# Two scaling multiplies of a memory attention: on VectorE in place of GpSimd

## Chip, cores and metric

One core of a Trainium2 chip runs the whole kernel. The metric is the device time of one execution in microseconds (us), lower is better. The core's engines, as the profile names them: PE (TensorE matmul; PEld its weight loads), DVE (VectorE), ACT (ScalarE), POOL (GpSimd) and SP (SyncE, which here only issues DMAs). Each engine works through its own queue in order and waits on semaphores for the others.

## What is computed

One layer of an encoder trunk on a sequence of 2048 tokens, 1024 channels, in float32. In the reference it has three parts: forgetting attention beside a multi-scale pool, then attention to 256 memory tokens, then a SwiGLU. The middle one matters here:

```python
hn = rmsnorm(h, g_mem_q)
mq = rmsnorm(head_split(hn @ w_mem_q, 4, 128), g_q_mem)      # queries, 4 heads of 128
sc = einsum('bshd,bmhd->bhsm', mq, mk) * 128 ** -0.5         # mk: 256 memory keys per head
pm = softmax(sc)
mo = einsum('bhsm,bmhd->bshd', pm, mv)
h = h + mo @ w_mem_out
```

## The kernel before

Float32 matmuls are made of three products of a high and a low word: a value x is split into `hi` (a rounded copy, written by ACT) and `lo = x - hi` (a subtraction on DVE, L55), and `mm3` issues hi·hi, hi·lo and lo·hi (L60 to L62). A DVE instruction on line L55 is therefore nearly always the second half of such a split, and the third matmul of a triple (L62) waits for it.

The memory attention takes the sequence in 16 tiles of 128 tokens, called 0 to 15 here. Tiles 0 and 1 begin in the stage before. From tile 2 on, one loop over n does in step n a piece of several tiles at once, in this order on PE:

- `query_norm` of tile n: 24 matmuls into a PSUM bank `mmps`. ACT scales it into `mq` (L1212) and squares it (L1214). DVE sums the squares per head (`ms`, L1216). POOL turns the four sums of each row into reciprocal roots `r` (L67, L71). Then `mq` is multiplied by `r`, 128x512 with `r` broadcast over each head (L1219).
- `ffn_turn` of tile n-5: PE transposes, DVE evicts them to `hst` (L1103), POOL stores `hst` (L1104).
- for every second n, `mem_values` of a pair of tiles (`mops`).
- the scores of tile n-1 (`scps`), then `softmax`: DVE takes the negated maxima `ng` (L1238), ACT four exponentials with their sums `l` (L1241), DVE the reciprocals of the sums (L1242), and `pm` is multiplied by them, 128x1024 with `l` broadcast over each head (L1243).
- `weights_tm` of tile n-2: eight transposes of `pm` (PE), high words by ACT (L1041), low words `pTl` by DVE (L55).
- `mem_out` of tile n-4, first half; DVE adds the residual (L1443).
- `tile_query` of tile n+1: eight transposes of `h`, whose high and low words go to one of three places named `hT`, `qs` and `kh` in turn. These are what `query_norm` of step n+1 reads.
- `mem_out`, second half, and last `query_t`: four transposes of the scaled `mq` of tile n.

The transposes use PSUM buffers `tp`, two in turn, and a transpose into a buffer waits until the DVE instruction that read it last is done. In the last steps the loop also takes in work of the stage behind it: sums of token blocks on DVE (`xraw`, L1074, with their splits into `qs`, `kh`, `kl`, `cb`) and of the first gate weights (`graw`, `t`, L1134), all from SBUF.

In this loop the orders of PE and SP are those of the code. DVE, ACT and POOL are ordered by a list scheduler when the kernel is built, so moving an instruction to another engine can move its neighbours.

Of the kernel before, what the change touches and what calls it, by code (L numbers as in the profile page):

```python
# [11 lines left out]
ALU = mybir.AluOpType  # L12
# [4 lines left out]
P = 128  # L17
# [9 lines left out]
MEM = 256  # L27
MH = 4
# [12 lines left out]
def block_kernel(ctx: ExitStack, tc: tile.TileContext, x, xT, memT, cols, rows, w_qkvf, w_p, w_pool, w_out,  # L41
# [4 lines left out]
    act, dve, pool, pe, sp = nc.scalar, nc.vector, nc.gpsimd, nc.tensor, nc.sync  # L46
# [10 lines left out]
    def mm3(ps, st, mv, first, last, goes_on=False):  # L57

        (sh, sl), (mh, ml) = st, mv
        pe.matmul(ps, lhsT=sh, rhs=mh, start=first, stop=False, skip_group_check=goes_on)  # L60
        pe.matmul(ps, lhsT=sh, rhs=ml, start=False, stop=False, skip_group_check=goes_on)  # L61
        pe.matmul(ps, lhsT=sl, rhs=mh, start=False, stop=last, skip_group_check=goes_on)  # L62

    def rsqrt(outp, ms, inv_n=None):

        if inv_n is not None:
            pool.tensor_scalar(out=ms, in0=ms, scalar1=inv_n, scalar2=EPS, op0=ALU.mult, op1=ALU.add)  # L67
        else:
            pool.tensor_scalar(out=ms, in0=ms, scalar1=EPS, scalar2=None, op0=ALU.add)
        n = ms.shape[-1]  # L70
        pool.tensor_tensor(out=outp, in0=ms, in1=mhalf[:, :n], op=ALU.pow)  # L71
# [1136 lines left out]
    def query_norm(ps, r, hTh, hTl):  # L1208
        for k in range(KD):
            mm3(ps, (hTh[:, k], hTl[:, k]), wq[k], k == 0, k == KD - 1)  # L1210
        mq = hp.tile([P, MH, P], F32, tag="cm", name="mq", bufs=3)
        act.activation(mq[:].rearrange("p h d -> p (h d)"), ps, AF.Copy, scale=r)  # L1212
        sq = hp.tile([P, MH, P], F32, tag="cm", name="mqsq", bufs=3)
        act.activation(sq[:], mq[:], AF.Square)  # L1214
        ms4 = stat.tile([P, MH], F32, tag="ms4", name="ms4", bufs=2)
        dve.tensor_reduce(out=ms4[:], in_=sq[:], axis=AX.X, op=ALU.add)  # L1216
        r4 = stat.tile([P, MH], F32, tag="r4", name="r4", bufs=2)
        rsqrt(r4[:], ms4[:], 1.0 / P)
        pool.tensor_tensor(out=mq[:], in0=mq[:], in1=r4[:].unsqueeze(2).to_broadcast([P, MH, P]), op=ALU.mult)  # L1219
        return mq  # L1220

    def query_t(mq, bank=tp_bank):
# [7 lines left out]
    def softmax(scs, pm, mqh, mql):  # L1230

        nh = MH // len(scs)
        sc = [s_[:, h] for s_ in scs for h in range(nh)]
        for h in range(MH):
            mm3(sc[h], (mqh[:, h], mql[:, h]), (mk[0][:, h], mk[1][:, h]), True, True)
        ng = stat.tile([P, MH], F32, tag="ng4", name="ng4", bufs=2)
        for n, s_ in enumerate(scs):
            dve.tensor_reduce(out=ng[:, n * nh:(n + 1) * nh], in_=s_, axis=AX.X, op=ALU.max, negate=True)  # L1238
        l4 = stat.tile([P, MH], F32, tag="l4", name="l4", bufs=2)
        for h in range(MH):  # L1240
            act.activation(pm[:, h], sc[h], AF.Exp, bias=ng[:, h:h + 1], scale=1.0, accum_out=l4[:, h:h + 1])  # L1241
        dve.reciprocal(l4[:], l4[:])  # L1242
        pool.tensor_tensor(out=pm[:], in0=pm[:], in1=l4[:].unsqueeze(2).to_broadcast([P, MH, MEM]), op=ALU.mult)  # L1243
        return pm

    with ExitStack() as c0:
# [98 lines left out]
        with in_order(EN.SP):  # L1345
# [46 lines left out]
            queries[1]()  # L1392
            mqd, qtd, pmd = {}, {}, {}
            mqd[0] = query_norm(banks[0], *qd.pop(0))
            earlier_1(*prev)
            mqd[1] = query_norm(banks[0], *qd.pop(1))
            qtd[0] = query_t(mqd.pop(0))
            pm0 = f(pair_place(6)[:]).rearrange("p a (h m) -> p (a h) m", m=MEM)
            pmd[0] = softmax([b_.rearrange("p (h m) -> p h m", m=MEM) for b_ in banks[1:]], pm0, *qtd.pop(0))
            queries[2]()  # L1400
            earlier_2(*prev)
            qtd[1] = query_t(mqd.pop(1))

    with mstack, ExitStack() as c0:
# [67 lines left out]
        with in_order(EN.SP):  # L1472
# [5 lines left out]
            for n in range(2, NT + 1):  # L1478
                if n < NT:
                    mqd[n] = query_norm(bigp.tile([P, 512], F32, tag="mm", name="mmps", bufs=2)[:], *qd.pop(n))  # L1480
# [16 lines left out]
                if 0 <= i < NT:  # L1497
                    pmd[i] = ptp.tile([P, MH, MEM], F32, tag="pm", name="pm", bufs=2)
                    softmax([bigp.tile([P, MH, MEM], F32, tag="sc", name="scps", bufs=1)[:]], pmd[i][:], *qtd.pop(i))
# [328 lines left out]
```

## Time and profile before

| | |
|---|---|
| median of 3 runs | 2586.41 us (2582.59 to 2586.48) |
| profiled execution, its own time | 2578.56 us |
| its span, first to last instruction | 2576.9 us |
| PE busy | 2510.7 us, 97% of the span |
| DVE busy | 1734.8 us, 67% |
| ACT busy | 1299.4 us, 50% |
| POOL busy | 822.0 us, 32% |
| the 16 `mq` multiplies (L1219), POOL | from 1024.9 to 1261.3 us of the span, 17.0 us in all |
| the 16 `pm` multiplies (L1243), POOL | from 1035.4 to 1277.2 us, 30.2 us in all |

Times within the execution are counted from the start of the span. Matmuls overlap in the pipe: a row's duration is longer than the distance to the next row's start, and the same holds, by less, for DVE rows that follow each other. The profiled execution took 7.85 us less than the median of the runs.

### The profile page before, as it was taken

The page shows a single profiled execution, that of the slowest core. Times are in us where ns is not written, and L with a number is a line of the kernel's source. Part 1 is how long each engine was busy: PE and PEld are TensorE (multiplying, and loading weights), DVE is VectorE, ACT ScalarE, POOL GpSimd, SP SyncE. Part 2 cuts the span into 40 slices and gives each one's busy share as a digit, 9 for nine tenths or more (in the row PEclk, how much of TensorE's full clock was granted, in tenths as well). Part 3 has the DMA queues.
Part 4 walks back from the last instruction along what each step waited for, and adds up shares of the span by engine and source line. Part 5 has one row for each costly group of instructions (what it writes and reads, how often), then busy time and mean ns, then how long its engine had stood idle before and what let it go on. Part 6 is the DMA issues. An engine that isn't in the chain of part 4 may idle for free.

```text
span 2576.9 us, 37301 instructions
## 1 busy us (share of the span) xinstructions
PE 2510.7 (97%) x12909; PEld 2154.4 (84%) x12909; DVE 1734.8 (67%) x2998; ACT 1299.4 (50%) x2487; POOL 822.0 (32%) x1135
## 2 busy tenths in 40 slices
PE   8999998999999899999999999999999999999998
PEld 8999997788887687888778888888888888888887
DVE  4466745899998754555877778756766666665554
ACT  5555446788889422655543433334543333333443
POOL 0022424455555522444424545430001222212000
PEclk9999999999999999999999999999999999999999
DMA  8755767645433546222465555447773323325665
GB/s 276 215 178 156 216 192 210 187 123 156 130 109 92 185 150 214 74 87 95 174 224 181 174 178 190 151 164 271 244 266 109 122 104 108 122 98 185 228 214 186
DMA packets 246766, 434.01 MB, mean 168 GB/s; under 512 B 30000, under 2 KB 119856, under 8 KB 238896
## 3 DMA queue, kind: packets, MB, share of 16 engines
q1 hardware_dynamic: 213104, 322.54, 39.5%
q0 software_dynamic: 33472, 109.08, 11.7%
q8 instruction: 102, 1.67, 0.3%
q14 instruction: 88, 0.72, 0.1%
HBM read 294.02 MB, written 137.50 MB: 167 GB/s over the span
## 4 chain that ended last, share of the span: by engine, by line
PE 49%; issue 8%; DVE 2%; ACT 1%; DMA 1%; POOL 1%; SPq 0%; POOLq 0%; DVEq 0%; ACTq 0%
PE bk L62 13%; PE bk L60 13%; PE bk L61 13%; PE mmps L60 2%; PE mmps L62 2%; PE mmps L61 2%; PE tp L1039 1%; DVE ww L55 0%; PE obk L60 0%; PE obk L61 0%; PE obk L62 0%; DMA xraw<-hTd 0%; POOL out_dram L1721 0%; DMA wqr<-in_w_mem_q_dram 0%; DMA h<-h1d 0%
## 5 line engine op out<-in xcount | busy, mean ns | idle before, releaser
L55 DVE TENSOR_TENSOR ww<-draw,ww 128x512 fp32r<-128x512 f32 x308 | 205.2, 702 | 155.6 <-ACT ww L199 155.1
L199 ACT CAST ww<-draw 128x512 fp32r<-128x512 f32 x308 | 179.5, 620 | 218.8 <-PE bk L62 174.5
L55 DVE TENSOR_TENSOR ww<-graw,ww 128x512 fp32r<-128x512 f32 x220 | 177.8, 815 | 105.9 <-ACT ww L199 105.5
L61 PE MATMUL bk<-ww,ww 128*128 128x512 f32 x616 | 239.6, 389 | 0.0
L60 PE MATMUL bk<-ww,ww 128*128 128x512 f32 x616 | 239.6, 389 | 0.0
L62 PE MATMUL bk<-ww,ww 128*128 128x512 f32 x616 | 239.6, 389 | 0.0
L199 ACT CAST ww<-graw 128x512 fp32r<-128x512 f32 x220 | 135.9, 622 | 181.8 <-PE bk L62 159.8
L55 DVE TENSOR_TENSOR pl<-tp,ph 128x512 fp32r<-128x512 f32 (+3 forms) x296 | 176.7, 599 | 27.8 <-ACT ph L952 26.0
L871 ACT ACTIVATE s<-s,mx 128x1024 f32<-128x1024 f32 (+2 forms) x192 | 173.6, 905 | 7.7 <-DVE mx L865 7.1
L936 PE MATMUL tp<-ident,s 128*128 128x128 f32 x1088 | 171.5, 273 | 3.4 <-DVE pl L55 3.0
L60 PE MATMUL zps<-wh,xhi 128*128 128x386 f32 x512 | 174.6, 341 | 0.0
L62 PE MATMUL zps<-wh,xl 128*128 128x386 f32 x512 | 173.7, 339 | 0.0
L61 PE MATMUL zps<-wl,xhi 128*128 128x386 f32 x512 | 173.2, 338 | 0.0
L952 ACT CAST ph<-tp 128x512 fp32r<-128x512 f32 (+3 forms) x296 | 148.7, 514 | 38.3 <-PE tp L936 32.8
L936 PEld LDWEIGHTS tp<-ident,s 128*128 128x128 f32 x1088 | 133.9, 141 | 31.6 <-DVE pl L55 6.6
L1721 POOL DMA_DIRECT2D out_dram<-o x32 | 17.3, 542 | 382.5 <-DVE o L1718 381.6
L62 PE MATMUL bk<-qs,ww 128*128 128x512 f32 x352 | 137.2, 390 | 1.1 <-DVE ww L55 1.1
L60 PE MATMUL bk<-qs,ww 128*128 128x512 f32 x352 | 137.9, 392 | 0.3 <-ACT s L1640 0.3
L61 PE MATMUL bk<-kh,ww 128*128 128x512 f32 x352 | 137.0, 389 | 0.0
L60 PE MATMUL bk<-kl,ww 128*128 128x512 f32 x352 | 136.9, 389 | 0.0
L61 PE MATMUL bk<-cb,ww 128*128 128x512 f32 x352 | 136.9, 389 | 0.0
L62 PE MATMUL bk<-kl,ww 128*128 128x512 f32 x352 | 136.9, 389 | 0.0
(613 smaller groups left out, 7261.9 us busy)
## 6 DMA issues: line engine op xcount, KB each, us to landing
graw<-in_w_gu_dram SPq DMA_DIRECT2D x44, 1024.0 KB, 5.4
draw<-in_w_down_dram SPq DMA_DIRECT2D x66, 256.0 KB, 4.3
xl<-in_xT_dram SPq DMA_DIRECT2D x64, 256.0 KB, 4.5
wdr<-in_w_down_dram SPq DMA_DIRECT2D x22, 512.0 KB, 4.6
jl<-in_x_dram SPq DMA_DIRECT2D x32, 256.0 KB, 7.0
vd<-cb SPq DMA_DIRECT2D x16, 512.0 KB, 3.5
cb<-cd SPq DMA_DIRECT2D x8, 1024.0 KB, 7.8
v<-vd SPq DMA_DIRECT2D x8, 1024.0 KB, 5.4
```

The lines of the kernel that those rows point to most:

```text
L55: (eng or dve).tensor_tensor(out=lo, in0=src, in1=f(hi), op=ALU.subtract)
L60: pe.matmul(ps, lhsT=sh, rhs=mh, start=first, stop=False, skip_group_check=goes_on)
L61: pe.matmul(ps, lhsT=sh, rhs=ml, start=False, stop=False, skip_group_check=goes_on)
L62: pe.matmul(ps, lhsT=sl, rhs=mh, start=False, stop=last, skip_group_check=goes_on)
L199: act.copy(hi, raw)
L871: act.activation(s[:, sl], s[:, sl], AF.Exp, bias=ng, scale=-1.0, accum_out=l[:, q, g:g + 1])
L936: pe.transpose(tp[:, q * P:(q + 1) * P], unit["rows"][q][:, j * P:(j + 1) * P], ident[:])
L952: act.copy(ph[:, sl], tp[:, sl])
L1039: pe.transpose(tp[:, e_], src[:, q + e_], ident[:])
L1721: pool.dma_start(out[rows_, cs], o)
```

## The change

Both multiplies are given to DVE instead of POOL; operands, shapes and places stay.

```diff
@@ query_norm
         rsqrt(r4[:], ms4[:], 1.0 / P)
-        pool.tensor_tensor(out=mq[:], in0=mq[:], in1=r4[:].unsqueeze(2).to_broadcast([P, MH, P]), op=ALU.mult)
+        dve.tensor_tensor(out=mq[:], in0=mq[:], in1=r4[:].unsqueeze(2).to_broadcast([P, MH, P]), op=ALU.mult)
         return mq
@@ softmax
         dve.reciprocal(l4[:], l4[:])
-        pool.tensor_tensor(out=pm[:], in0=pm[:], in1=l4[:].unsqueeze(2).to_broadcast([P, MH, MEM]), op=ALU.mult)
+        dve.tensor_tensor(out=pm[:], in0=pm[:], in1=l4[:].unsqueeze(2).to_broadcast([P, MH, MEM]), op=ALU.mult)
         return pm
```

The reciprocal roots `r` are still made on POOL. The orders of PE and SP are the same as before. POOL loses 32 instructions. DVE gains 32, and the scheduler puts them as follows.

DVE at tile 3, as it stands with the change (`wm30l` is the low word of a weight, `qs` are the low words that `query_norm` of tile 4 reads):

```order
L1216 TENSOR_REDUCE ms_13219<-mqsq 128x4
L55 TENSOR_TENSOR wm30l<-wmr,wm30h 128x512
L1219 TENSOR_TENSOR mq<-mq,r_13221 128x512
L1238 TENSOR_REDUCE ng_13241<-scps 128x4
L55 TENSOR_TENSOR pTl<-tp_13250,pTh 128x4x128
L55 TENSOR_TENSOR pTl<-tp_13257,pTh 128x4x128
L55 TENSOR_TENSOR qs<-tp_13271,qs 128x512
L55 TENSOR_TENSOR qs<-tp_13278,qs 128x512
```

The `mq` multiply is new in this list; all else stands as before, now behind it. At tile 2 it stands behind `ng` and ahead of the two `pTl` and of `hT`.

DVE at tile 11, one of the tiles with odd numbers in the even part of the loop (5, 7, 9, 11 and 13 read alike), the difference:

```order
 L1216 TENSOR_REDUCE ms_14551<-mqsq 128x4
 L1103 TENSOR_TENSOR hst<-tp_14565,gffn 128x512
+L1219 TENSOR_TENSOR mq<-mq,r_14553 128x512
 L1238 TENSOR_REDUCE ng_14589<-scps 128x4
 L55 TENSOR_TENSOR pTl<-tp_14598,pTh 128x4x128
 L55 TENSOR_TENSOR pTl<-tp_14605,pTh 128x4x128
+L1443 TENSOR_TENSOR h_13352<-mmps,h_13352 128x512
 L1242 RECIPROCAL l_14591<-l_14591 128x4
-L1443 TENSOR_TENSOR h_13352<-mmps,h_13352 128x512
+L1243 TENSOR_TENSOR pm<-pm,l_14591 128x1024
 L55 TENSOR_TENSOR hT<-tp_14633,hT 128x512
 L55 TENSOR_TENSOR hT<-tp_14640,hT 128x512
```

`mq` now stands ahead of `ng`, and `pm` ahead of the low words of the next tile's `hT`.

DVE at tile 15, the last query, the difference:

```order
 L1103 TENSOR_TENSOR hst<-tp_15241,gffn 128x512
 L1216 TENSOR_REDUCE ms_15235<-mqsq 128x4
-L55 TENSOR_TENSOR kh<-xraw,qs 128x512
+L1238 TENSOR_REDUCE ng_15290<-scps 128x4
+L1219 TENSOR_TENSOR mq<-mq,r_15237 128x512
 L1103 TENSOR_TENSOR hst<-tp_15249,gffn 128x512
-L1238 TENSOR_REDUCE ng_15290<-scps 128x4
 L55 TENSOR_TENSOR pTl<-tp_15299,pTh 128x4x128
```

`ng` and `mq` have come between the sum of squares and the second `hst`, and a `kh` has gone from there to a place earlier.

## Prediction

> **What bounds the kernel.** I read the page first, then the busy time in the stretch that holds the two multiplies, then PE's own waits there.
>
> ```profile
> PE 2510.7 (97%) x12909; PEld 2154.4 (84%) x12909; DVE 1734.8 (67%) x2998; ACT 1299.4 (50%) x2487; POOL 822.0 (32%) x1135
> ...
> 1062.00:1244.00 182.00, 181.00 (x1069) 157.50 (x1067) 95.81 (x142) 104.15 (x225) 83.87 (x116) 1.00 0.29 97
> 1244.00:1300.00 56.00, 49.26 (x270) 40.31 (x269) 49.27 (x74) 29.09 (x65) 22.76 (x29) 1.00 0.57 203
> ```
>
> The last two rows give, after the length, busy us of PE, PEld, DVE, ACT and POOL, then the granted clock. PE is the bound of the whole kernel. From 1062 to 1244 it leaves 1.0 us of 182 free, with DVE only 53% busy; from 1244 to 1300 it leaves 6.7 us, and DVE is the busiest engine beside it (88%). The clock is 1.00 in both, so only PE's waits can change. PE's waits from 1000 to 1320 (total us, times, longest):
>
> ```profile
> PE tp L1039 <- POOL mq L1219: 3.6, 2, 2.0
> PE tp L1039 <- DVE hst L1103: 2.8, 6, 1.8
> PE mmps L60 <- DVE ww L1443: 2.2, 1, 2.2
> ...
> PE tp L1039 <- POOL hr L71: 1.2, 1, 1.2
> ...
> PE tp L1102 <- DVE pTl L55: 0.8, 1, 0.8
> ```
>
> PE waits for `mq` only twice in 16 tiles, and never for `pm`. The gain can't be 16 times anything; what counts is what the two instructions delay on DVE.
>
> **Prices of the moved instructions.** The POOL rows of the multiplies, and a DVE row of the stage before with the same form as `pm` (128x1024 by a broadcast factor from POOL):
>
> ```profile
> L1243 POOL TENSOR_TENSOR pm<-pm,l 128x1024 f32<-128x1024 f32 x15 | 28.3, 1890 | 26.8 <-PE mmps L62 18.3 <-DVE l L1242 8.5
> L1219 POOL TENSOR_TENSOR mq<-mq,r 128x512 f32<-128x512 f32 x16 | 17.0, 1060 | 1.3
> ...
> L411 DVE TENSOR_TENSOR cb<-kh,zrq 128x1024 f32<-128x1024 f32 x8 | 9.8, 1222 | 7.7 <-POOL zrq L71 7.7
> ```
>
> So `pm` costs 1.22 us on DVE against 1.89 on POOL, and `mq` 0.68 (the 128x512 rows below) against 1.06. In a run of DVE rows the next starts after 0.60 (128x512) or 1.13 (128x1024), and these are what a queue pays. For the step from POOL to DVE and from DVE to PE I take 0.07 us each (at tile 15 below, `hst` ends at 1260.64 and PE starts at 1260.70). POOL gets 47 us back (17.0 and 30.2); apart from `mq`, PE waits for POOL only in the one row on `hr`, which is taken up below, so this relief is costed at nothing by itself.
>
> **Tile 2.** The rows around PE's first wait, by engine:
>
> ```profile
> 1045.27 1.03 POOL L71 TENSOR_TENSOR r<-ms,mhalf 128x4 f32<-128x4 f32 x1
> 1044.81 1.21 DVE L1238 TENSOR_REDUCE ng<-scps 128x4 f32<-128x1024 f32 x1
> 1045.94 1.28 DVE L55 TENSOR_TENSOR pTl<-tp,pTh 128x512 fp32r<-128x512 f32 x2
> 1047.14 0.68 DVE L55 TENSOR_TENSOR hT<-tp,hT 128x512 fp32r<-128x512 f32 x1
> 1047.47 0.66 PE L1039 MATMUL tp<-ident,mq 128*128 128x128 f32 x4 [1.64 <-POOL mq L1219]
> 1048.42 0.39 PE L62 MATMUL mmps<-qs,hT 128*128 128x512 f32 x1
> ```
>
> `r` ends at 1046.30, so `mq` runs on DVE from 1046.37 to 1047.05 and PE starts its transposes at 1047.12: 0.35 earlier. But DVE stands still from 1045.94 until `r` comes, and both `pTl` and `hT` are behind `mq`: `hT` begins at 1046.37 + 3 x 0.60 = 1048.17 and ends at 1048.85. The third matmul of the next tile (L62, 1048.42) needs it, so it starts at 1048.92. The gain is gone and PE is **0.5 us later**.
>
> **Tile 3.** The same with `mq` ahead of `ng` too:
>
> ```profile
> 1056.57 1.01 POOL L71 TENSOR_TENSOR r<-ms,mhalf 128x4 f32<-128x4 f32 x1
> 1056.35 1.22 DVE L1238 TENSOR_REDUCE ng<-scps 128x4 f32<-128x1024 f32 x1
> 1058.68 1.28 DVE L55 TENSOR_TENSOR qs<-tp,qs 128x512 fp32r<-128x512 f32 x2
> 1058.75 0.66 PE L1039 MATMUL tp<-ident,mq 128*128 128x128 f32 x4 [1.97 <-POOL mq L1219]
> 1059.71 0.39 PE L62 MATMUL mmps<-qs 128*128 128x512 f32 x1
> ```
>
> `r` ends at 1057.58, `mq` runs from 1057.65, PE's transposes gain 0.35 again. `ng` waits from 1056.35 to 1058.25, then 1.13 for `ng` and 2 x 0.60 for `pTl` put `qs` at 1060.58 to 1061.26, and the L62 matmul of tile 4 at 1061.33 in place of 1059.71: **1.6 us later**.
>
> **Tiles 4 to 13.** In even tiles `r` comes while DVE is idle or in a split with slack; I cost them at nothing, because the matmuls of `mem_values` and of the scores stand on PE between and hide `mq`; without that cover they would cost what an odd tile costs. The same holds for tiles 0 and 1, for whose `mq` PE does not wait now. In odd tiles `ng` waits for `r`:
>
> ```profile
> 1188.04 1.04 POOL L71 TENSOR_TENSOR r<-ms,mhalf 128x4 f32<-128x4 f32 x1
> 1188.13 1.21 DVE L1238 TENSOR_REDUCE ng<-scps 128x4 f32<-128x1024 f32 x1
> 1191.53 1.04 PE L1039 MATMUL tp<-ident,h 128*128 128x128 f32 x8
> ```
>
> `mq` starts at 1189.15, `ng` at 1189.75 (1.6 late), the two `pTl` at 1190.88 and 1191.48, the second ending at 1192.16. PE's eight transposes of `h` reuse the two `tp` buffers that the `pTl` free. The first four, at 1191.53, would wait 0.1, the second four, at 1191.97, up to 0.26. The cover of 1.6 us is just used up. Between 0 and 0.26 I take 0.14 for each of five odd tiles, since the margin is that of my hops: **0.7 us**. `pm` lands in idle time: the exponentials and the `hT` behind them move with `ng`, and the transposes of `mq` at the end of the step still find `hT` done. If that cover is gone, each `pm` is worth at most its 1.13 us.
>
> **From 1238 on** DVE is nearly full, and two effects work against each other. Rows:
>
> ```profile
> 1238.26 1.04 POOL L71 TENSOR_TENSOR r<-ms,mhalf 128x4 f32<-128x4 f32 x1
> 1246.13 2.60 DVE L1074 TENSOR_TENSOR xraw<-xraw 128x512 f32<-128x512 f32 x1
> 1246.26 1.91 POOL L1243 TENSOR_TENSOR pm<-pm,l 128x1024 f32<-128x1024 f32 x1
> 1248.65 1.28 DVE L55 TENSOR_TENSOR hT<-tp,hT 128x512 fp32r<-128x512 f32 x2
> 1249.47 0.63 PE L1039 MATMUL tp<-ident,mq 128*128 128x128 f32 x4 [1.22 <-POOL hr L71]
> 1249.85 0.68 DVE L1074 TENSOR_TENSOR xraw<-xraw 128x512 f32<-128x512 f32 x1
> ...
> 1239.72 1.53 DVE L55 TENSOR_TENSOR cb<-xraw,kl 128x512 fp32r<-128x512 f32 x1
> 1264.76 1.86 DVE L55 TENSOR_TENSOR kh<-xraw,qs 128x512 fp32r<-128x512 f32 x1
> 1277.51 2.10 DVE L55 TENSOR_TENSOR cb<-xraw,kl 128x512 fp32r<-128x512 f32 x1
> ```
>
> The same `xraw` subtraction takes 0.68 us alone and 2.60 while POOL's `pm` (1246.26 to 1248.17) runs: a DVE instruction with two operands in SBUF stands still as long as POOL's multiply works. Four such rows lose 1.92, 0.85, 1.18 and 1.42 us over 0.68, 5.4 in all. The change ends these and pays 3 x 1.13 + 2 x 0.60 = 4.6 on DVE. [...]
>
> *Before 1249.47:* PE waits for a `tp` buffer that `hT` frees (ended 1249.33). With the change `mq` begins when `r` is there, at 1239.37, and from it to `hT` DVE has eleven instructions at 0.60 (`mq`, two `ww`, two `kh`, `cb`, two `pTl`, two `xraw`, `h`), two at 1.13 (`ng`, `pm`) and a reciprocal at 0.1: 9.0 us. That puts `hT` at 1248.3 in place of 1248.65: **-0.3 us**. The `hr` that the list names ended at the same moment; without `pm` ahead of it on POOL it comes earlier too.
>
> *Tile 15.* The second `hst` frees the `tp` buffer for `pm`:
>
> ```profile
> 1259.96 0.68 DVE L1103 TENSOR_TENSOR hst<-tp,gffn 128x512 f32<-128x512 f32 x1
> 1260.18 1.04 POOL L71 TENSOR_TENSOR r<-ms,mhalf 128x4 f32<-128x4 f32 x1
> 1260.70 0.65 PE L1039 MATMUL tp<-ident,pm 128*128 128x128 f32 x4 [1.75 <-DVE hst L1103]
> ```
>
> Now it stands behind `mq`, and so behind `r`, which ends at 1261.22: `mq` at 1261.29, `hst` at 1261.89 to 1262.57, PE at 1262.64: **+1.9 us**.
>
> *1261 to 1291:* two blocked rows (1.18 + 1.42) go and two `pm` (2 x 1.13) come. DVE's work is 0.3 us less. PE arrives 1.9 later by the step before, while its waits here come to 1.5 at most (the 6.7 us left free, less 1.2, 1.8 and 2.2 of the rows for `hr`, `hst` and L1443; the longest is the 0.8 for `pTl`): they can go, no more. Between 0 and -1.5 I take **-1.0**, since the delay is longer than the waits.
>
> *The end of the stage:*
>
> ```profile
> 1294.92 0.69 DVE L1134 TENSOR_TENSOR t<-graw,t 128x512 f32<-128x512 f32 x1 [3.00 <-DMA hTd<-hst]
> 1297.33 1.28 DVE L1443 TENSOR_TENSOR ww<-mmps,ww 128x512 f32<-128x512 f32 x2
> 1298.07 0.50 PE L60 MATMUL mmps<-wm00h,ww 128*128 128x512 f32 x1 [2.18 <-DVE ww L1443]
> ```
>
> DVE waits 3.0 us for a store, then does four instructions, then the L1443 that PE waits for. In the new order six stand between, 1.2 us more, if the store moves with PE (it holds `hst`, which follows PE's transposes). If it hangs on other stores of POOL's queue instead, PE is late enough to find it landed, and loses its 2.2 of waiting. Between -2.2 and +1.2 I take **0**, near the middle, as no row decides.
>
> **Sum:** 0.5 + 1.6 + 0.7 - 0.3 + 1.9 - 1.0 + 0 = +3.4 us. The profiled execution's span goes from 2576.9 to 2580.3 and its time from 2578.56 to about 2582.0; the median lies 7.85 above that execution, which gives 2589.8. A difference under 0.2% (5.2 us) can't be told from none here, so the forecast is no measurable change, leaning to slower.
>
> **Rivals.** [...] PE's 6.7 free us from 1244 to 1300 hang on DVE or on what DVE delays. If the 5.4 us that DVE gets back remove them all and tile 15 costs nothing, the sum is 0.5 + 1.6 + 0.7 - 6.7 = -3.9: 2582.5. For it: the four long rows. Against: `hst` of tile 15 waits for `r` whatever DVE's load. It decides if `r` of tile 15 is ready by 1260. [...] *C, every step gains.* If each multiply were on PE's path, 16 x (1.06 - 0.68) + 16 x (1.89 - 1.22) = 16.8 us would go: 2569.6. The list of waits speaks against it: two of 32 are. [...]
>
> **How the numbers follow.** Forecast 0.60, A 0.13 (0.03 of it beyond -0.2%), B 0.22, C 0.05. Faster is C and the tail of A, 0.08; slower is B, 0.22; the rest, 0.70, is the same. The range goes from just under A, 2582.0, to B, 2595.0; left out are C, the tail of A and about half of B, 0.19. The forecast's own range is 2586.4 to 2591.6.
>
> **What would show it.** L1219 and L1243 on DVE at about 0.68 and 1.22 us; no PE wait for `mq` from POOL, but waits at L62 for `hT` and `qs` of 0.5 to 2 us at tiles 2 to 4; `ng` of odd tiles behind a DVE wait for `r`; no `xraw` row over 1 us from 1240 to 1280; PE's wait for `hst` at tile 15 near 3.5 us. The forecast is wrong if the L62 waits stay away, if PE's waits from 1249 to 1298 vanish, or if they grow beyond 10 us.

## The result: 0.23% slower, and where it went

Over twelve runs each the changed kernel takes 2590.79 us (2582.71 to 2594.62) and the kernel before 2584.66 us (2580.55 to 2589.65). The ratio is 1.0023, with a 95% interval of 1.0015 to 1.0032: 6.1 us slower, where 3.4 us were forecast. The forecast time was 2589.8 us, which looks closer than it is: it stood on a median of before that was 1.75 us above the one of twelve runs. So the difference is what has to be explained.

The page of the changed kernel, its line of busy times, and below it the two stretches of the loop (length, busy us of PE, PEld, DVE, ACT and POOL, granted clock, DMA). The second stretch is a little longer than the one of before, since everything comes later:

```profile
PE 2516.2 (97%) x12909; PEld 2157.6 (83%) x12909; DVE 1754.6 (68%) x3030; ACT 1300.5 (50%) x2487; POOL 777.7 (30%) x1103
...
1062.00:1244.00 182.00, 179.83 (x1047) 154.59 (x1048) 109.86 (x161) 105.43 (x229) 54.90 (x93) 1.00 0.27 89
1244.00:1310.00 66.00, 58.10 (x312) 48.79 (x311) 54.55 (x86) 32.59 (x71) 17.86 (x27) 0.95 0.59 211
```

POOL is 44 us lighter and DVE 20 us heavier, and that decides nothing. Two things do: PE leaves more time free, and the granted clock of the second stretch is 0.95 where it was 1.00. The two instructions themselves, by group (count, busy us, mean ns, then the idle time of DVE just before them):

```profile
L1243 DVE TENSOR_TENSOR pm<-pm,l 128x1024 f32<-128x1024 f32 x15 | 18.4, 1224 | 0.4
L1219 DVE TENSOR_TENSOR mq<-mq,r 128x512 f32<-128x512 f32 x16 | 11.1, 692 | 13.2 <-POOL r L71 13.2
```

Both cost what was forecast (1.22 and 0.69 us, for 1.22 and 0.68). `pm` finds its operand ready. Ahead of `mq` DVE stands still for 13.2 us in all, and whatever is queued behind it stands too. PE's waits from 1000 to 1330 show who that was:

```profile
PE tp L1039 <- DVE hst L1103: 4.6, 7, 3.2
PE mmps L60 <- DVE ww L1443: 3.1, 1, 3.1
PE tp L1039 <- DVE mq L1219: 2.9, 2, 1.6
PE mmps L62 <- DVE qs L55: 1.7, 1, 1.7
...
PE tp L1039 <- DVE hT L55: 0.8, 1, 0.8
...
PE mmps L62 <- DVE hT L55: 0.6, 1, 0.6
```

The waits for `mq` are shorter than those for POOL's `mq` (2.9 for 3.6). In exchange PE waits for `hT` (0.6, at L62) and `qs`, which it did not before, and longer for `hst` (4.6 us for 2.8).

**Tile 3** in the rows of DVE, POOL and PE:

```profile
1058.42 1.01 POOL L71 TENSOR_TENSOR r<-ms,mhalf 128x4 f32<-128x4 f32 x1
1059.46 0.69 DVE L1219 TENSOR_TENSOR mq<-mq,r 128x512 f32<-128x512 f32 x1 [1.18 <-POOL r L71]
1060.07 1.22 DVE L1238 TENSOR_REDUCE ng<-scps 128x4 f32<-128x1024 f32 x1
1061.21 1.28 DVE L55 TENSOR_TENSOR pTl<-tp,pTh 128x512 fp32r<-128x512 f32 x2
1062.40 1.28 DVE L55 TENSOR_TENSOR qs<-tp,qs 128x512 fp32r<-128x512 f32 x2
1063.14 0.50 PE L62 MATMUL mmps<-qs 128*128 128x512 f32 x1 [1.74 <-DVE qs L55]
```

DVE idles 1.18 us for `r`; `ng`, `pTl` and `qs` follow, and PE waits 1.74 us at the third matmul of tile 4, where 1.6 had been worked out.

**Tile 15**, where the second `hst` frees PE's `tp` buffer, and the first matmuls behind it:

```profile
1264.58 1.04 POOL L71 TENSOR_TENSOR r<-ms,mhalf 128x4 f32<-128x4 f32 x1
1265.65 0.69 DVE L1219 TENSOR_TENSOR mq<-mq,r 128x512 f32<-128x512 f32 x1 [0.70 <-POOL r L71]
1266.26 0.68 DVE L1103 TENSOR_TENSOR hst<-tp,gffn 128x512 f32<-128x512 f32 x1
1267.10 1.08 PE L1039 MATMUL tp<-ident,pm 128*128 128x128 f32 x4 [3.20 <-DVE hst L1103]
...
1268.40 0.63 PE L61 MATMUL mmps<-wm00l,ww 128*128 128x512 f32 x1
1268.83 0.63 PE L62 MATMUL mmps<-wm00h,ww 128*128 128x512 f32 x1
1269.26 0.63 PE L60 MATMUL mmps<-wm10h,ww 128*128 128x512 f32 x1
```

The wait of 3.20 us is the forecast one. What was not forecast stands below it: these 128x512 matmuls start 0.43 us apart, while the same matmuls elsewhere in this stage start 0.227 apart. The stretches around this wait and around the one at the stage's end, in periods of 3.41 us (columns as above):

```profile
1262.96:1266.37 3.41, 0.66 (x4) 0.42 (x4) 2.71 (x5) 2.11 (x9) 1.99 (x3) 1.00 0.98 380
1266.37:1269.79 3.42, 2.69 (x9) 2.34 (x10) 3.42 (x6) 2.16 (x6) 1.37 (x2) 0.50 0.93 342
1300.50:1303.92 3.42, 0.83 (x4) 0.37 (x2) 3.42 (x7) 1.24 (x2) 0.00 (x0) 1.00 1.03 379
1303.92:1307.33 3.41, 2.93 (x7) 2.35 (x8) 1.02 (x2) 0.00 (x0) 0.55 (x1) 0.50 1.01 386
```

In the first and third row PE was busy for 0.66 and 0.83 of 3.41 us. In the next 3.41 us the granted clock is exactly half. No such stretch lies between 973 and 1330 in the profiled execution of before.

**The account by stretch.** The distance on PE between the same two matmuls, after less before, from 1036 to 1326 of before. The clock's part is half of the time that PE worked at half clock; it is taken out of the four stretches and stands by itself.

| kernel (profiled execution) | 1036-1062 | 1062-1244 | 1244-1292 | 1292-1326 | without clock | clock |
|---|---|---|---|---|---|---|
| the change | +2.1 | +1.2 | -0.7 | +0.9 | +3.6 | +2.8 |
| forecast | +2.1 | +0.7 | +0.6 | 0 | +3.4 | none |

So in this execution the queue cost what was forecast, and the clock came on top: 6.4 us together, 6.1 in the medians. The split is not exact, since a PE that the clock has delayed waits less elsewhere. The kernel e11 below has the same order of work up to 1292, and half-clock stretches at tiles 2 and 3 that cost it 4.8 us; its first three columns are +1.8, +1.0 and -1.5, so the queue's part up to 1292 is between 1.4 and 2.7 us.

The clock's part does not rest on single executions alone, because the granted clock of every run is on record. One less the clock, times the span, is the time that the clock takes if PE works all the while. In the mean it is 19.5 us over 35 runs of before and 23.5 over the twelve of the change, 4.0 more with an uncertainty of 1.0. In the half-clock rows above PE worked 2.69 and 2.93 us of 3.41, so about four fifths of that, some 3 us (an estimate), are lost time of PE.

### The profile page after: what moved, and what is told of

Same layout as the page of the kernel before. It is cut to its first block, busy times and chain, and to the rows that moved or that the text cites. A ratio compares the mean times of both kernels' runs of the same rounds, so it can differ in the third digit from the quotient of the medians.

```text
span 2585.5 us, 37240 instructions
## 1 busy us (share of the span) xinstructions
PE 2516.2 (97%) x12909; PEld 2157.6 (83%) x12909; DVE 1754.6 (68%) x3030; ACT 1300.5 (50%) x2487; POOL 777.7 (30%) x1103
## 4 chain that ended last, share of the span: by engine, by line
PE 49%; issue 9%; DVE 2%; POOL 1%; ACT 1%; DMA 1%; POOLq 0%; DVEq 0%; ACTq 0%
PE bk L62 13%; PE bk L61 13%; PE bk L60 13%; PE mmps L62 2%; PE mmps L60 2%; PE mmps L61 2%; PE tp L1039 1%; DVE ww L55 0%; PE obk L60 0%; DMA wqr<-in_w_mem_q_dram 0%; PE obk L61 0%; PE obk L62 0%; POOL out_dram L1721 0%; DVE hst L1103 0%; ACT mq L1212 0%
## 5 line engine op out<-in xcount | busy, mean ns | idle before, releaser
L62 PE MATMUL bk<-ww,ww 128*128 128x512 f32 x616 | 239.6, 389 | 0.0
L62 PE MATMUL zps<-wh,xl 128*128 128x386 f32 x512 | 173.7, 339 | 0.0
L62 PE MATMUL bk<-qs,ww 128*128 128x512 f32 x352 | 137.2, 390 | 1.2 <-DVE ww L55 1.2
L62 PE MATMUL bk<-kl,ww 128*128 128x512 f32 x352 | 136.9, 389 | 0.0
L61 PEld LDWEIGHTS bk<-ww,ww 128*128 128x128 f32 x616 | 115.6, 188 | 24.4 <-DVE ww L55 0.4
```

## The experiments

Two theories for the loss. *Q, the queue:* DVE works in order and stands still for POOL's `r`; the loss is what stands behind `mq`. *L, the load:* the loss is DVE's added work, two thirds of it `pm`. For the second half of the loss a third theory, *K, the clock*, with what speaks for and against it below. In the tables "measured" is the ratio to the kernel before with its 95% interval, and in us of 2584; the stretches are as above.

**One multiply at a time.** The first kernel moves only `mq`, the second only `pm` (each is before with one line of the change).

```diff
-        pool.tensor_tensor(out=mq[:], in0=mq[:], in1=r4[:]...)    # first kernel: mq only
+        dve.tensor_tensor(out=mq[:], in0=mq[:], in1=r4[:]...)
-        pool.tensor_tensor(out=pm[:], in0=pm[:], in1=l4[:]...)    # second kernel: pm only
+        dve.tensor_tensor(out=pm[:], in0=pm[:], in1=l4[:]...)
```

Expected of `mq` alone:

> Only the multiply of mq (L1219) goes to VectorE; that of pm (L1243) stays on GpSimd. Theory Q (queue): the loss of the whole change comes from VectorE standing still for r in its in-order queue, so this half alone loses: the waits of PE for hT at tile 2 and qs at tile 3 (0.6 and 1.7 us in the whole change) and the one of about 3.2 us for hst at tile 15 stay, the long xraw and kh rows from 1240 on stay too; +4 to +6 us, ratio 1.0015 to 1.0025. Theory L (load): the loss is VectorE's added work, 16 x 0.60 us here against 16 x 1.13 us of the other half, so about a third of the +6.1 us, +2 us, ratio 1.0008.

Expected of `pm` alone:

> Only the multiply of pm (L1243) goes to VectorE; that of mq (L1219) stays on GpSimd. Theory Q: nothing new waits for r on VectorE, the rows that the multiply of pm held up (1.92, 1.18 and 1.42 us) go, PE's wait for hst at tile 15 is at most 1.8 us; -1 to -3 us, ratio 0.999 to 1.000. Theory L: two thirds of the loss, +4 us, ratio 1.0016.

| kernel | measured | 1036-1062 | 1062-1244 | 1244-1292 | 1292-1326 | without clock | clock |
|---|---|---|---|---|---|---|---|
| `mq` only | 1.0024 (1.0014 to 1.0034), +6.2 | +1.1 | +1.1 | +1.2 | 0.0 | +3.5 | +3.4 |
| `pm` only | 1.0006 (0.9997 to 1.0014), +1.5 | +0.6 | -0.1 | -0.9 | +1.6 | +1.3 | +3.4 |

`mq` alone loses as much as both, and L's 1.0008 lies outside its interval. That settles for Q. `pm` alone did not gain the 1 to 3 us that Q gave it. The +0.6 of its first stretch is a queue too: the first of the 16 multiplies of `pm` now stands ahead of two `kh`, and PE waits 0.57 us for these at 1040.30. PE's longest waits of that kernel from 1244 to 1310 show where they stayed:

```profile
PE mmps L60 <- DVE ww L1443: 3.9, 1, 3.9
PE tp L1039 <- DVE hst L1103: 1.8, 1, 1.8
```

The wait at tile 15 keeps its 1.8, the 0.9 us are gained up to 1292, and the stage's end gives them back: its wait grows from 2.18 to 3.9 us. DVE gets its `t` there only after 3.66 us of waiting for the store, and then six instructions stand ahead of L1443, as in the changed kernel, instead of four.

**The last tile.** The whole change, with `mq` of tile 15 left on POOL.

```diff
-    def query_norm(ps, r, hTh, hTl):
+    def query_norm(ps, r, hTh, hTl, eng=None):
-        dve.tensor_tensor(out=mq[:], ...)
+        (eng or dve).tensor_tensor(out=mq[:], ...)
-   mqd[n] = query_norm(..., *qd.pop(n))
+   mqd[n] = query_norm(..., *qd.pop(n), pool if n in (15,) else dve)
```

> The whole change, but the multiply of mq of the last tile (15) stays on GpSimd. Theory Q: hst no longer stands behind r there; PE's wait for it falls from 3.2 to about 1.8 us and the matmuls behind it are 227 ns apart in place of 427: -3 us against the whole change, +3 us against before, ratio 1.0012. Theory L: one 0.60 us instruction in 32 fewer, no measurable difference from the whole change, ratio 1.0023.

Measured: 1.0019 (1.0009 to 1.0028), +4.9 us. Stretches +2.0, +1.0, -2.1, +0.8, without the clock +1.7. PE's longest waits there, from 1244 to 1310:

```profile
PE mmps L60 <- DVE ww L1443: 3.1, 1, 3.1
PE tp L1039 <- DVE hst L1103: 2.2, 2, 1.8
```

The ratio decides nothing here, as its interval holds the 1.0012 of Q and the 1.0023 of L; the trace does. The wait for `hst` fell to 1.8, and 1244 to 1292 got 1.4 us faster than with the whole change, as Q says. The other half of the expectation missed: the matmuls behind the 1.80 us wait ran at half clock all the same (a stretch from 1272.1 to 1275.5). So a half-clock stretch needs no single wait as long as those of 3.20 and 3.07 us: here 0.36 us of waiting at 1268.94 and the 1.80 lie in one period of 3.41 us.

**Late.** Both multiplies on DVE, but `mq` is multiplied where its transposes are, at the start of `query_t`.

```diff
     def query_norm(...):
-        dve.tensor_tensor(out=mq[:], ...)
-        return mq
+        return mq, r4
     def query_t(mq, ...):
+        mq, r4 = mq
+        dve.tensor_tensor(out=mq[:], ...)
```

> Both multiplies on VectorE, but that of mq is written where its transposes are (start of query_t) in place of the end of query_norm, so that in odd tiles it stands behind ng and both pTl, and at tile 15 behind hst and both pTl; even tiles keep the order of the whole change but for tile 2, where it stands behind hT. Theory Q: the loss of the odd tiles and of tile 15 with its slow matmuls goes, tile 3 keeps some; 0 to +2 us, ratio 1.0000 to 1.0008. Theory L: the same 32 instructions run on VectorE, so +6 us, ratio 1.0023.

Measured: 1.0005 (0.9996 to 1.0013), +1.3 us, with the same 32 multiplies on DVE: L is out. Stretches +1.9, 0.0, -3.1, +0.4, without the clock -0.8. The loss of the odd tiles and of tile 15 is gone. What is left stands at tiles 2 and 3, where `mq` now waits behind `ng`, the splits and the reciprocals. PE's wait for the `mq` of tile 2, which is put down to the instruction ahead of it:

```profile
PE tp L1039 <- DVE l L1242: 2.7, 1, 2.7
```

So the next version keeps the `mq` of these two tiles on POOL, early, and all others late on DVE.

```diff
     def query_norm(..., eng=None):
+        if eng:
+            eng.tensor_tensor(out=mq[:], ...)
+        return mq, None if eng else r4        # query_t multiplies if r4 is given
-   mqd[n] = query_norm(..., *qd.pop(n))
+   mqd[n] = query_norm(..., *qd.pop(n), pool if n in (2, 3) else None)
```

> As the late version (mq multiplied on VectorE at the start of query_t), but the mq of tiles 2 and 3, for which PE stood waiting, is multiplied on GpSimd in query_norm as before. Theory Q (queue): the 1.9 us that tiles 2 and 3 cost beside the clock in the late version go, the 3.1 us that it gains from 1244 to 1292 stay, the end of the stage costs up to 1 us: -1 to -3 us against before without the clock, ratio 0.999 to 1.000. Theory L (load): 30 of the 32 multiplies still run on VectorE, about +6 us, ratio 1.002.

Measured: 0.9997 (0.9989 to 1.0005), -0.8 us. Stretches -0.3, 0.0, -2.2, +0.4, without the clock -2.1: this is most likely the relief of DVE's long rows, with little against it. No run isolates it: `pm` alone, which ends the longest of them, gained 0.9 in that stretch. The time by itself is not told from before, but L's 1.002 is out again. DVE's row of these multiplies, from 1000 to 1330:

```profile
L1226 DVE TENSOR_TENSOR mq<-mq,r 128x512 f32<-128x512 f32 x14 | 9.6, 688 | 6.7 <-POOL r L71 6.7
```

DVE still stands 6.7 us for `r` in all. It costs nothing, because nothing that PE is about to wait for stands behind it.

**The clock.** The half-clock stretches of all profiled executions begin on a grid of 3.413 us that is fixed within an execution and lies elsewhere from one to the next. In before they begin at 416.24, 457.20, 856.56 and 969.20, the last three 12, 129 and 162 periods behind the first; in the kernel with `pm` alone (e2) one begins at 1062.66, in the late version with tiles 2 and 3 on POOL (e6) at 1060.63, which is 0.6 of a period ahead of it. Counted over 13 executions, in periods that began at full clock: every one in which PE idled 1.95 us or more (of 3.41) was followed by a period at half clock, none with less than 1.73 was, and between the two it went either way (1.89 us from 1057.22 in e6 was followed by one, 1.94 us from 1010.97 in `mq` alone, e1, was not). A half-clock period in which PE idled 0.75 us or more was followed by a second one, one with less than 0.6 was not; the two nearest in the traces of before and the change: 0.76 us from 856.56 in before was, 0.73 us from 1266.37 in the change was not. A pair shows what the grid does. The rows of the changed kernel stand above: a wait of 3.20 us, one period with 0.66 us of PE work, half clock. Here is the same wait in a kernel that is told of below, the whole change with nine filling matmuls (e11), whose order is the same up to this place. First PE's rows, then the two periods of its grid:

```profile
1271.36 0.63 PE L1039 MATMUL tp<-ident,pm 128*128 128x128 f32 x4 [3.21 <-DVE hst L1103]
...
1272.28 0.39 PE L62 MATMUL mmps<-wm00h,ww 128*128 128x512 f32 x1
1272.51 0.40 PE L60 MATMUL mmps<-wm10h,ww 128*128 128x512 f32 x1
```

```profile
1266.30:1269.71 3.41, 1.73 (x13) 1.28 (x12) 2.86 (x4) 1.73 (x5) 1.82 (x3) 1.00 0.85 309
1269.71:1273.13 3.42, 1.77 (x10) 1.60 (x11) 3.22 (x7) 3.15 (x10) 0.99 (x2) 1.00 0.99 317
```

The grid cuts the same wait in two, PE idles 1.7 us or less in each of the two periods, and the matmuls behind it are 0.23 us apart. So the length of a pause does not decide by itself: 1.80 us with a shorter pause beside it brought a half-clock stretch, and 3.21 us did not.

Laid over all positions of the grid, PE's pauses from 1020 to 1340 cost an estimated 1 to 2 us a run in the kernel before and 3 to 6 in the changed one. The estimate hangs on the idle time at which the clock is taken to drop (1.75 to 1.95 us) and on whether second periods are counted; taken the same way in both kernels, the difference is 2 to 4 us. With the queue's +3.6 that makes 5.6 to 7.6 us for the change, 6.1 measured.

To try K, PE was given useless work ahead of its long waits: the first product of a group is computed two or three times more, before the group itself.

```diff
         def product_o(ps, xop, wop, first, fill=0):
+            for _ in range(fill):
+                mm3(ps, (xop[0][:, :P], xop[1][:, :P]), ob[wop, 0], True, True)
-   product_o(b, cur["s1"], "t1", True)
+   product_o(b, cur["s1"], "t1", True, {1: 3, 5: 2, 7: 2}.get(p_, 0))
         def mem_out(i, h1, mo, a):
+            for _ in range(3 if (i, a) == (NT - 2, 1) else 0):
+                mm3(ps[:], (mo[0][:, 0, ts], mo[1][:, 0, ts]), (wm[0, a][0][:], wm[0, a][1][:]), True, True)
```

On the whole change (e7):

> The whole change, and on PE 6 or 9 matmuls of 227 ns more just ahead of four of its long waits: the first product of the matmul group before the wait is computed up to three times more (start flag set, so the sums stay what they are): in the pair stage before the waits at 891, 972 and 1012 us, and in mem_out of tile 14 before the wait of 3.07 us at 1304. Theory K (clock): the granted clock halves for one period of 3.41 us after a period in which PE idled about 1.95 us or more; the filled waits are shorter than that, no half-clock stretch follows them, and it is about 4 us (2.5 x 1.6) faster than the whole change, ratio to before about 1.0008. If the clock has another cause, PE has 6.8 us more work that is hidden in its waits: no difference, ratio 1.0023, or slower.

On the late version with tiles 2 and 3 on POOL (e8):

> The late version with tiles 2 and 3 on GpSimd and the same filling matmuls as in the whole change with fill. Theory K: about 4 us faster than without the fill, ratio to before 0.997 to 0.999, which would be the fastest kernel here. Without an effect of the fill: as without it, 0.999 to 1.000.

On the kernel before (e9):

> The kernel before with the same filling matmuls and no multiply moved. Theory K: no half-clock stretch after the waits at 889, 969, 1012 and 1298 us; 3 to 4 us faster, ratio 0.9985 to 0.999. If the clock has another cause: ratio 1.000 or above.

Measured: 1.0042 (1.0030 to 1.0054), 1.0003 (0.9994 to 1.0012) and 1.0016 (1.0008 to 1.0025): the first and the third are 11 and 4 us slower than before, the second 1.6 us slower than without the fill. The expectation failed, and not by the clock: half-clock stretches remained in the pair stage, but behind other waits. In the pair stage of the kernel before with fill, DVE from 888 on:

```profile
888.41 1.28 DVE L1328 TENSOR_TENSOR o<-obk,o 128x512 f32<-128x512 f32 x2
894.34 0.69 DVE L55 TENSOR_TENSOR ww<-praw,ww 128x512 fp32r<-128x512 f32 x1 [4.65 <-ACT ww L199]
896.26 0.69 DVE L55 TENSOR_TENSOR ww<-praw,ww 128x512 fp32r<-128x512 f32 x1 [1.23 <-ACT ww L199]
896.87 0.68 DVE L1333 TENSOR_TENSOR o<-obk,o 128x512 f32<-128x512 f32 x1
```

And PE's longest waits from 880 to 1000, the first row with the fill, the second the kernel before (its L1326 is L1328 with the fill):

```profile
PE obk L60 <- DVE o L1333: 6.5, 2, 3.8
```

```profile
PE obk L60 <- DVE o L1326: 6.6, 3, 3.0
```

In before the scheduler had placed this sum `o` (L1333 here, L1331 there) at 891.80, ahead of the splits; with two microseconds more on PE it put two splits that wait for ACT ahead of it, and PE waited for the sum instead. The waits at 889 and 973 did shrink, to 1.0 and 1.6 us, but new ones of 2.7 and 3.8 us came one or two products later. It is Q once more, by another door. At the end of the stage, where DVE's queue kept its order, the nine matmuls were hidden whole: 1292 to 1326 costs -0.2, -0.1 and -0.3 us in the three kernels, with no half-clock stretch behind. That is the test of K by an edit: of the seven profiled kernels without these nine matmuls six have a half-clock stretch behind this wait (all but before), of the six with them none.

So the last three kernels have only these nine (the second half of the diff). The late version (e10):

> The late version with tiles 2 and 3 on GpSimd, and of the filling matmuls only the nine in mem_out of tile 14, ahead of PE's wait at the end of the stage; the pair stage keeps the order of before. Theory K (clock): that wait gets about 2 us shorter at no cost, no half-clock stretch follows it, and the 2.1 to 2.5 us that this version gained beside the clock show: -3 us against before, ratio 0.9985 to 0.9993. If the fill costs its 2.0 us: ratio 1.000 or above.

The whole change (e11):

> The whole change with only the nine filling matmuls in mem_out of tile 14. Theory K: the wait of 3.07 us at 1304 falls to about 1 us, the half-clock stretch behind it goes, that behind the wait of 3.20 us at tile 15 stays; 1 to 2.5 us faster than the whole change, ratio to before 1.0013 to 1.0019. If the stretches do not hang on the waits, it stays (ratio 1.0023); if the fill costs its 2.0 us, ratio 1.003.

The kernel before (e12):

> The kernel before with only the nine filling matmuls in mem_out of tile 14 and no multiply moved. If the gain of 3 us of the late version with this fill comes mostly from the moved multiplies (2.1 us by its traces from 1244 to 1292), the fill alone gains 0 to 1 us here, where PE's wait is 2.18 us and is followed by a half-clock stretch in about half the executions: ratio 0.9996 to 1.000. If the fill is the whole gain: ratio 0.9988.

The "about half the executions" is an estimate: a pause of 2.18 us puts 1.95 us or more into one period of 3.41 us at half of the grid's positions.

| kernel, with nine filling matmuls | measured | without clock | clock |
|---|---|---|---|
| late, tiles 2 and 3 on POOL | 0.9988 (0.9980 to 0.9997), -3.1 | -1.0 | 0 |
| the whole change | 1.0022 (1.0013 to 1.0031), +5.7 | +1.8 | +4.8 |
| before | 0.9999 (0.9990 to 1.0008), -0.3 | -0.2 | +1.7 |

The late version with the fill is the fastest kernel here, 3.1 us under before and, by the ratios, 9 under the change. Its lead over before is clear of the noise by little: the interval ends at 0.9997. Its stretch from 1244 to 1292 gains the same 2.2 us as without the fill; the stage's end costs it 1.3 in this execution. Its waits from 1244 to 1310:

```profile
PE tp L1039 <- DVE hst L1103: 2.2, 2, 1.8
PE mmps L60 <- DVE ww L1449: 1.4, 1, 1.4
```

The fill alone gives 0.3 us and the late multiplies alone 0.8, both within their uncertainty, so how the 3.1 us divide is not settled. On the whole change the 1 to 2.5 us that were expected of the fill did not come. Its trace shows the wait at the end cut to 0.6 us and no half clock there, but this execution's grid fell on the pauses of tiles 2 and 3 instead (4.8 us of clock in all). Why the runs are hardly faster stays open; over all of them the clock takes 22.3 us in place of 23.5, which can't be told from nothing. In the late version with tiles 2 and 3 on POOL the nine matmuls do raise the clock: it takes 16.8 us in the mean of its runs, 21.3 without them and 19.5 in before (uncertain by less than 1 each). K is shown, by the count and by the edit, as the cause of the half-clock stretches; that shortening pauses saves the estimated time is not shown by a ratio.

## Why the prediction was right and where it was off

- *Tile 2, +0.5, and tile 3, +1.6:* +0.5 and +1.6. Right in place, cause and size.
- *Odd tiles, +0.7, five times 0.14 between 0 and 0.26:* +1.2, at the upper end. Four more kernels with `mq` ahead of `ng` show +1.0 to +1.1; those without it show -0.1 to 0.0 (before with the pair-stage fill shows +0.7, all of it at the matmul that ends the stretch). The rows of tile 11:

```profile
1193.43 0.69 DVE L1219 TENSOR_TENSOR mq<-mq,r 128x512 f32<-128x512 f32 x1 [0.83 <-POOL r L71]
1194.04 1.22 DVE L1238 TENSOR_REDUCE ng<-scps 128x4 f32<-128x1024 f32 x1
...
1195.91 0.42 PEld L1039 LDWEIGHTS tp<-ident,h 128*128 128x128 f32 x4 [0.27 <-DVE pTl L55]
...
1196.51 0.42 PEld L1039 LDWEIGHTS tp<-ident,h 128*128 128x128 f32 x4 [0.18 <-DVE pTl L55]
```

- *Before 1249.47, -0.3:* -0.5.
- *Tile 15, +1.9:* +2.1, and the wait of "near 3.5" is 3.20.
- *1261 to 1291, -1.0, at most -1.5:* -2.1. The account of the blocked rows held: no `xraw`, `kh` or `cb` row from 1242 to 1300 is over 0.8 us each, where four of before, from 1239 on, took 1.5 to 2.6. Beside POOL's multiplies the rows of before with an operand in PSUM kept their length: two `pTl` took 1.28 us together from 1045.94 (`mq` from 1046.38), `h` 0.69 at 1264.15 (`pm` from 1264.18). The bound failed. It was made of the time PE left free, and a PE row's idle time starts at a modelled end that overlaps the next start. In before:

```profile
1289.87 0.40 PE L61 MATMUL mmps<-wm00l,ww 128*128 128x512 f32 x1
1290.60 0.50 PE L62 MATMUL mmps<-wm00h,ww 128*128 128x512 f32 x1 [0.33 <-DVE ww L55]
```

The row names 0.33 us, but the matmul starts 0.73 after the one ahead of it, where 0.23 is usual: 0.50 are lost. The 0.80 of `pTl` at 1285.68 were 0.96. Counted by starts, some 2.1 us were lost in this stretch, and they went.
- *The end of the stage, 0 between -2.2 and +1.2:* +0.9 without the clock. The six instructions do stand behind the store, DVE's wait for it is as long as before, and PE's wait grew from 2.18 to 3.07:

```profile
1300.04 0.69 DVE L1134 TENSOR_TENSOR t<-graw,t 128x512 f32<-128x512 f32 x1 [2.85 <-DMA hTd<-hst]
...
1303.66 1.28 DVE L1443 TENSOR_TENSOR ww<-mmps,ww 128x512 f32<-128x512 f32 x2
```

- *The step that failed:* "The clock is 1.00 in both, so only PE's waits can change." The waits change the clock. The price was in no term: 2.8 us in this execution and some 3 by the clocks of all runs (an estimate, worked out above), about the difference between 3.4 and 6.1. The profiled execution of before did show it, earlier in the kernel (clock 0.50 from 416.24, 457.20, 856.56 and 969.20), but I had read only the stretches of the change. The execution that the prediction was worked out from also had an unusually high clock: 0.995, or 12.9 us, where the clock takes 19.5 in the mean of the runs of before. So a good part of the 7.85 us between that execution and the median was clock as well.
- *The forecast as a whole:* the direction and the mechanism of the queue are borne out. That its sum fits so well (+3.6 for +3.4) is luck in part, as the misses of +0.5, -1.1 and +0.9 nearly cancel. That 2590.79 lies inside the forecast's own range of 2586.4 to 2591.6 owes something to luck: 6.1 us on the median it started from would have been 2592.5. And "no measurable change" is not borne out, as the interval of 1.0015 to 1.0032 leaves 1 out.
- *The rivals:* A, 2582.5, gave the 5.4 us of DVE's long rows back to PE. That most likely shows in the two late versions (-2.2 to -3.1 us from 1244 to 1292), but in the change tile 15 costs what it brings, as the condition on `r` said. B, 2595.0, the top of the range, had DVE as the bound, with 8.6 us lost and nothing gained back. No run shows those 8.6 us: the long rows went, and POOL's shorter work had not held DVE up in before, where three `xraw` rows took 2.13 us together from 1252.91, beside `fms` and `fr` (1253.06 to 1254.74) and a DMA issue (1254.71). DVE's load as the bound is out by the late version (the same 32 multiplies, +1.3 us). C is out; and a multiply takes 1.55 times as long on POOL as on DVE (1.06 for 0.68 us, 1.89 for 1.22).

## What to carry to other kernels

An instruction that is moved to a less loaded place in another engine's queue takes its wait with it: price what stands behind it there, and write it where nothing that the bottleneck needs soon stands behind it. Here moving the line, and leaving two of sixteen tiles where they were, undid the loss of 6 us, although half of DVE's 13.2 us of standing still remained. Work that is "free" because an engine waits can still change another engine's order (here the sum `o` went from 891.80 to 896.87), so look at the order again after adding it. And read PE's losses from the distance of starts, not from the idle time of the row alone (0.50 us lost at 1290.60, where the row names 0.33).

## What was not expected of the hardware

In these executions PE's granted clock halved for one grid period of 3.41 us, at times two, after a period with some 1.9 us or more of idle PE. That cost up to 1.7 us a period (half of the 3.41 us that PE worked from 969.20 in before), and the grid's place differed from execution to execution. One pause of 3.2 us cost 1.3 us in one execution (the change, 2.69 us of PE work at 0.50) and nothing in another (e11). The 12 runs of before spread over 9 us (2580.55 to 2589.65). By PE's pauses in the traces the clock costs an estimated 0 to 3.4 us of an execution of before from 1020 to 1340, and 2.4 to 7.2 from 840 to 1020, by the grid's place alone.
